# Rounding and splitting the weights by DMA instead of by compute engines, in a hybrid attention and ConvFFN layer

## The chip, the cores and the metric

The kernel runs on one core of a Trainium2 chip. The metric is the device time of one execution in microseconds (us). TensorE (PE in the rows) multiplies; VectorE (DVE), ScalarE (ACT) and GpSimd (POOL) do the elementwise work; SyncE (SP) issues the DMAs, which 16 DMA engines carry out.

## What is computed

One layer of a streaming encoder, on 512 prompt tokens and 32 sample tokens, 544 columns in all:

```python
h = rmsnorm(x, n1)
z = h @ w_in          # q_a | k_a | v_a | q_b | k_b | v_b | gate_a | gate_b
# mixer A: sliding-window attention with sinks; mixer B: chunk-band attention with a bias table
x = x + (sigmoid(gate_a) * o_a + sigmoid(gate_b) * o_b) @ w_out
u = rmsnorm(x, n2) @ w_up
c = conv_b + conv_w[0] * up[:, 0:t] + conv_w[1] * up[:, 1:t+1] + conv_w[2] * up[:, 2:t+2]
a, g = split(c)
x = x + (gelu(a) * g) @ w_down
```

All inputs and outputs are float32; D_MODEL is 1024 and D_FF is 2816.

## The kernel before

**Products in three passes.** The products run on TensorE in a rounded 32-bit type (fp32r). To keep the accuracy of float32, each operand is split into a high half (the value rounded to fp32r) and a low half (the value minus its high half, rounded again), and each product is three matmuls: high times high, high times low, low times high (`triple`, L220). A weight here is one tile of 128 partitions by 1024 elements, 512 KB: one block of 128 output rows over all 1024 inputs. Its product with the activations takes 8 (blocks of the inner dimension) times 2 (halves of the 544 columns, 272 each) times 3, so 48 matmuls.

**Which weights there are.** `sources` lists 110 of them: 52 of `w_in`, 8 of `w_out`, 44 of `w_up` and 6 of `w_down` (the part of `w_down` called `rest`). `ffn` is 60, the number of the first `w_up` weight. The rest of `w_down` is read as `w_pair` by `sums` (L1007), which forms the sums that a fast product of 2 by 2 blocks needs.

**How a weight is prepared.** `prep` (L192) loads the raw tile by a DMA that SP issues, rounds it into `w_hi` (on GpSimd in L201 while `n < ffn`, on ScalarE in L203 after that), and subtracts on VectorE into `w_lo` (L204). The raw tile, `w_hi` and `w_lo` have two buffers each. `weights` (L213) hands out the next weight and sees that the two after it have been asked for (`n + 3`). All of `prep` is traced at a low priority (`LATER`), so the scheduler places its instructions where an engine has nothing more urgent at that point of its plan; the order on each engine is fixed when the kernel is built.

**Stages.** Until about 30 us the input is loaded and normed and the first three weights are used. From there to about 480 us the `w_in` products alternate with attention: each head's norm (`head_norm`, L401), softmax (L478), transposes (`transposed`, L504) and its products are threaded between the dense matmuls by `Stream`, at places that were planned with the constants `LAT_...` and `PACE_...`. Then come `w_out` (to about 520 us), the ConvFFN's `w_up` products, two weights for each tile of the gated value (to about 790 us), the `rest` products (to about 830 us) and the fast product from `sums` (to the end).

**The FFN's pairs.** `make_pair` (L960) splits and sums two gated tiles for the fast product; the first `EARLY` of the 8 pairs are made inside the gate loop, the others after it (L1002).

Of the kernel before, what the change touches and what calls it, by code (L numbers as in the profile page):

```python
# [8 lines left out]
F32 = mybir.dt.float32  # L9
F32R = mybir.dt.float32r  # L10
AF = mybir.ActivationFunctionType
ALU = mybir.AluOpType
# [14 lines left out]
GT = FF // 128  # L27
PAIRS = 8
REST = GT - 2 * PAIRS
EARLY = 5  # L30
UNITS = PAIRS // 2
H = T // 2
EPS = 1e-6
# [24 lines left out]
LAT_SOFT_S, LAT_PTS = 8.46, 1.1  # L58
PACE_A, PACE_B, PACE_S = 7.09, 5.87, 1.44

WARM = 7
START = "x0a w0 x0b x1 w1 x2 w0 x3 w1 x4 x5 x6 x7"
FIRST = 3
# [80 lines left out]
def body(ctx, tc, a, o):  # L144
    nc = tc.nc
    pe = Stream(nc)
    mm, transpose = pe.matmul, pe.transpose
    act = nc.scalar.activation
    V, G = nc.vector, nc.gpsimd
    rr = lambda t: t.bitcast(F32)  # L150

    const = ctx.enter_context(tc.tile_pool(name="const", bufs=1))
    wp = ctx.enter_context(tc.tile_pool(name="wp", bufs=2))
# [12 lines left out]
    def load(out, src, kind="x"):  # L166

        with tc.issue_after(loads[kind].ins) if kind in loads else nullcontext():
            loads[kind] = nc.sync.dma_start(out=out, in_=src)
# [13 lines left out]
    sources = [a["w_in"][m] for m in plan] + [a["w_out"][m] for m in range(8)]  # L183
    ffn = len(sources)
# [4 lines left out]
    W = {}  # L189
    state = {"prepped": 0, "used": 0}  # L190

    def prep(n):  # L192
        raw = wp.tile([128, 1024], F32, name="w_raw", bufs=2)
        hi = wp.tile([128, 1024], F32R, name="w_hi")
        lo = wp.tile([128, 1024], F32R, name="w_lo")
        W[n] = (hi, lo)
        cuts = (0, 256, 1024) if n < 2 else (0, 1024)
        for c in map(slice, cuts, cuts[1:]):
            load(raw[:, c], sources[n][:, c])
            if n < ffn:  # L200
                G.tensor_scalar(hi[:, c], raw[:, c], 1.0, 1.0, ALU.mult, ALU.mult)  # L201
            else:
                nc.scalar.copy(hi[:, c], raw[:, c])  # L203
            V.tensor_tensor(lo[:, c], raw[:, c], rr(hi)[:, c], ALU.subtract)  # L204
            yield

    def prep_next():
        with tc.high_priority(LATER):
            for _ in prep(state["prepped"]):
                pass  # L210
        state["prepped"] += 1

    def weights():  # L213
        n = state["used"]
        state["used"] += 1
        while state["prepped"] < min(n + 3, len(sources)):
            prep_next()
        return W.pop(n)

# [12 lines left out]
    def dense(evac, pool=None):  # L232
        if not norm_done:
            return dense_first(evac)
        if early:
            pool = psa
            early.clear()
        w = weights()
        for s, (c0, cn) in enumerate(HALVES):
            ps = bank(pool or psd)  # L240
            for k in range(KC):
                triple(ps, w, k, c0, cn, k == 0, k == KC - 1)
                if k == KC - 1:
                    evac(s, c0, cn, ps[:, :cn])
                if xt:
                    rescale(state["used"], s, k)
                pe.step()
# [23 lines left out]
    def dense_first(evac):  # L271


        early.append((evac, weights()))
        if len(early) < (FIRST if xt else 2):
            return
        halves = [(bank(psd if i < 3 else psa), early[i // 2][1], i % 2) for i in range(2 * len(early))]
        interleaved(halves[:3], range(KC))
        for h in halves[3:]:
            interleaved([h], range(KC))  # L280
        while not norm_done:
            pe.idle()
        for i, (ps, _, s) in enumerate(halves):
            c0, cn = HALVES[s]
            early[i // 2][0](s, c0, cn, ps[:, :cn])
# [80 lines left out]
    att = ctx.enter_context(ExitStack())  # L366
# [5 lines left out]
    V.memset(rr(zeros)[:, :512], 0.0)  # L372
    for i in range(WARM):
        mm(warm, lhsT=zeros[:, :128], rhs=zeros[:, :512], start=i == 0, stop=i == WARM - 1)

    xt = [slot() for _ in range(KC)]
    load(n1, a["n1"])
    w = [prep(0), prep(1)]
    for step in START.split():
        n = int(step[1])  # L380
        if step[0] == "w":
            next(w[n])
        else:
            c = {"": slice(0, T), "a": slice(0, HALVES[0][1]), "b": slice(HALVES[0][1], T)}[step[2:]]
# [485 lines left out]

    lag = 2
    w0, w1 = weights(), weights()
    halves = [(bank(psd), w0, 0), (bank(psd), w0, 1), (bank(psd), w1, 0), (bank(psa), w1, 1)]
    for k in range(KC):
# [8 lines left out]
    interleaved(halves[3:], range(KC))  # L883
    att.close()

    fp = att.enter_context(tc.tile_pool(name="fp", bufs=50, reuse_waits="tile"))
    ft = att.enter_context(tc.tile_pool(name="ft", bufs=1, reuse_waits="tile"))
    x1 = [fp.tile([128, T], F32, name="s") for _ in range(KC)]
    for m in range(KC):
# [63 lines left out]
    rest, pairs = [], []  # L953
    homes = [gp] * 19 + [fp] * (7 * EARLY + 2 * REST - 19) + [f"x{p}{k}" for k in range(KC) for p in "hl"]

# [4 lines left out]
    def make_pair(v1, v2):  # L960
        b11, b12, b21, b22 = (v[:, c:c + H] for v in (v1, v2) for c in (0, H))
        t13, t24 = (fp.tile([128, T], F32, name="s") for _ in range(2))
        first, *wide = home(), (home(), home()), (home(), home()), (home(), home())
        nc.scalar.copy(first[:, :H], b11)
        V.tensor_tensor(first[:, H:], b11, rr(first)[:, :H], ALU.subtract)
        split(*wide[0], v2)
        V.tensor_tensor(t13[:, :H], b11, b12, ALU.subtract)
        V.tensor_tensor(t13[:, H:], b12, b22, ALU.subtract)
        split(*wide[1], t13)
        V.tensor_tensor(t24[:, :H], b22, t13[:, :H], ALU.add)  # L970
        V.tensor_tensor(t24[:, H:], b21, t24[:, :H], ALU.subtract)
        split(*wide[2], t24)
        ops = {"b11": (first[:, :H], first[:, H:])}
        for names, hl in zip((("b21", "b22"), ("t1", "t3"), ("t2", "t4")), wide):
            for e, name in enumerate(names):
                ops[name] = tuple(x[:, e * H:e * H + H] for x in hl)
        pairs.append(ops)

    late = []
    for n, i in enumerate(gate_order):  # L980
# [6 lines left out]
        def gate(c, part=part, n=n):  # L987
# [7 lines left out]
            late.append(v)  # L995
            if n % 2 and len(pairs) < EARLY:
                make_pair(*late)
# [8 lines left out]

    def sums():  # L1007
        for n in range(KC // 2 * UNITS):
            raw = wp.tile([128, 1024], F32, name="w_raw", bufs=2)
            load(raw, a["w_pair"][n])  # L1010
            wc, wd, wa, wb = (raw[:, 256 * e:256 * e + 256] for e in range(4))
            s13, s24 = (fp.tile([128, 2, 256], F32, name="s") for _ in range(2))
            s1, s3, s2, s4 = s13[:, 0], s13[:, 1], s24[:, 0], s24[:, 1]
            V.tensor_tensor(s13, raw[:, 256:768].rearrange("p (e c) -> p e c", e=2),
                            wc.unsqueeze(1).to_broadcast([128, 2, 256]), ALU.add)
            V.tensor_tensor(s2, s1, wa, ALU.add)
            V.tensor_tensor(s4, s2, wb, ALU.add)
            for x in (wa, s2, s3, s1, wb, wd, s4):
                w = fp.tile([128, 2, 256], F32R, name="s")
                nc.scalar.copy(w[:, 0], x)  # L1020
                V.tensor_tensor(w[:, 1], x, rr(w)[:, 0], ALU.subtract)
                ready.append(w)
                yield

    ready = []
    making = sums()

    def operand(n, ahead=10):
# [9 lines left out]
    def block(n):  # L1038
        if n // 8 not in held:
            held[n // 8] = weights()  # L1040
        hi, lo = held[n // 8]
        ks = slice(128 * (n % 8), 128 * (n % 8) + 128)
        return hi[:, ks], lo[:, ks]

    for m in range(KC):
        ps = [bank(psa if m % 2 else psd) for _ in HALVES]
        for k in range(REST):
            for s, (c0, cn) in enumerate(HALVES):
                hi, lo = block(m * REST + k)
# [182 lines left out]
```

## Time and profile before

| | us |
|---|---|
| median of 3 runs | 924.47 (922.49 to 924.73) |
| the profiled execution | 924.88 |
| its span, from the first to the last instruction | 923.0 |

| engine | busy us | share of the span | instructions |
|---|---|---|---|
| PE | 898.6 | 97% | 7085 |
| DVE | 723.6 | 78% | 1471 |
| ACT | 542.2 | 59% | 1285 |
| POOL | 379.1 | 41% | 578 |

Of the profiled execution, 1.9 us lie around its span. Busy time of TensorE is the time in which at least one of its matmuls is under way; they overlap, so the mean duration of one (292 ns) is longer than the distance from one to the next. A share over the whole span is a mean of stages with different limits, so the stages are read one by one.

### The profile page before, as it was taken

The page shows a single profiled execution, that of the slowest core. Times are in us where ns is not written, and L with a number is a line of the kernel's source. Part 1 is how long each engine was busy: PE and PEld are TensorE (multiplying, and loading weights), DVE is VectorE, ACT ScalarE, POOL GpSimd, SP SyncE. Part 2 cuts the span into 40 slices and gives each one's busy share as a digit, 9 for nine tenths or more (in the row PEclk, how much of TensorE's full clock was granted, in tenths as well). Part 3 has the DMA queues.
Part 4 walks back from the last instruction along what each step waited for, and adds up shares of the span by engine and source line. Part 5 has one row for each costly group of instructions (what it writes and reads, how often), then busy time and mean ns, then how long its engine had stood idle before and what let it go on. Part 6 is the DMA issues. An engine that isn't in the chain of part 4 may idle for free.

```text
span 923.0 us, 18908 instructions
## 1 busy us (share of the span) xinstructions
PE 898.6 (97%) x7085; PEld 884.4 (96%) x7085; DVE 723.6 (78%) x1471; ACT 542.2 (59%) x1285; POOL 379.1 (41%) x578
## 2 busy tenths in 40 slices
PE   8879999999999999999999999999999999999998
PEld 7879899989989999999999999999999999999998
DVE  7799876868888888998866558768777776886996
ACT  5568777778878777777764244344444443534542
POOL 6534457465876777766541103221222221100100
PEclk9999999999999999999999999999999999999999
DMA  6222222322334443434415222222222222332342
GB/s 216 83 82 88 71 90 85 101 81 75 109 118 122 135 124 109 129 110 136 133 59 168 89 92 92 92 77 85 92 93 92 84 87 83 96 101 81 119 145 67
DMA packets 40012, 94.38 MB, mean 102 GB/s; under 512 B 4944, under 2 KB 16240, under 8 KB 39920
## 3 DMA queue, kind: packets, MB, share of 16 engines
q1 hardware_dynamic: 39920, 93.17, 31.8%
q8 instruction: 56, 0.92, 0.4%
q14 instruction: 36, 0.29, 0.1%
HBM read 80.48 MB, written 7.10 MB: 95 GB/s over the span
## 4 chain that ended last, share of the span: by engine, by line
PE 76%; DVE 9%; ACT 4%; POOL 3%; issue 2%; DMA 0%; DVEq 0%; POOLq 0%
PE ps L85 73%; PE ps L89 3%; ACT p L485 2%; DVE q L446 1%; DVE zn L422 1%; DVE p L501 1%; DVE w_lo L204 1%; POOL p L493 1%; DVE s L254 1%; DVE t_b L319 1%; DVE k L431 1%; POOL t_sql L414 1%; POOL z L421 1%; DVE pt_l L512 0%; DMA k<-k 0%
## 5 line engine op out<-in xcount | busy, mean ns | idle before, releaser
L85 PE MATMUL ps<-xh,w_lo 128*128 128x272 f32 x1536 | 446.3, 292 | 5.1 <-DVE w_lo L204 5.1
L85 PE MATMUL ps<-xh,w_hi 128*128 128x272 f32 x1536 | 446.0, 292 | 2.7 <-ACT z L412 1.7
L85 PE MATMUL ps<-xl,w_hi 128*128 128x272 f32 x1536 | 446.3, 291 | 0.8 <-DVE xl L327 0.8
L85 PEld LDWEIGHTS ps<-xh,w_lo 128*128 128x128 f32 x1536 | 291.6, 190 | 6.5 <-DVE w_lo L204 6.0
L85 PEld LDWEIGHTS ps<-xh,w_hi 128*128 128x128 f32 x1536 | 291.5, 190 | 4.8 <-ACT z L412 1.9
L85 PEld LDWEIGHTS ps<-xl,w_hi 128*128 128x128 f32 x1536 | 292.0, 190 | 2.1 <-DVE xl L327 1.7
L204 DVE TENSOR_TENSOR w_lo<-w_raw,w_hi 128x1024 fp32r<-128x1024 f32 (+2 forms) x112 | 143.2, 1279 | 30.8 <-ACT w_hi L203 18.3
L201 POOL TENSOR_SCALAR w_hi<-w_raw 128x1024 fp32r<-128x1024 f32 (+2 forms) x62 | 66.6, 1075 | 90.2 <-PE ps L85 70.3
L493 POOL TENSOR_SCALAR p<-p,rc 128x256 f32<-128x256 f32 (+3 forms) x128 | 74.2, 596 | 41.4 <-DVE rc L491 38.0
L203 ACT CAST w_hi<-w_raw 128x1024 fp32r<-128x1024 f32 x50 | 52.6, 1051 | 64.9 <-issue 36.1
L85 PE MATMUL ps<-s,w_hi 128*128 128x272 f32 x448 | 84.0, 288 | 0.0
L485 ACT ACTIVATE p<-p,nm 128x256 f32<-128x256 f32 (+3 forms) x128 | 65.4, 514 | 27.8 <-DVE nm L482 27.7
L938 POOL TENSOR_SCALAR state_u<-u 128x2 f32<-128x2 f32 x44 | 17.1, 388 | 148.7 <-DVE u L935 148.7
L85 PE MATMUL ps<-s 128*128 128x272 f32 (+1 forms) x483 | 71.3, 293 | 1.7 <-DVE s L372 1.7
L85 PEld LDWEIGHTS ps<-s,w_hi 128*128 128x128 f32 x448 | 70.1, 188 | 0.0
L935 DVE TENSOR_TENSOR u<-ps,rstd 128x272 f32<-128x272 f32 x88 | 38.5, 441 | 39.6 <-PE ps L85 37.0
L85 PEld LDWEIGHTS ps<-s 128*128 128x128 f32 x483 | 65.1, 190 | 2.2 <-DVE s L372 1.7
L85 PE MATMUL ps<-s,w_lo 128*128 128x272 f32 x224 | 63.8, 288 | 0.0
L85 PE MATMUL ps<-k,q 128*128 128x256 f32 (+2 forms) x256 | 52.1, 308 | 3.5 <-DMA k<-k 1.8
L414 POOL TENSOR_TENSOR t_sql<-t_sq,t_sqh 128x272 fp32r<-128x272 f32 x52 | 52.7, 1014 | 3.7
L421 POOL TENSOR_TENSOR z<-z,t_y 128x272 f32<-128x272 f32 x52 | 42.7, 822 | 23.9 <-ACT t_y L316 21.7
L512 DVE TENSOR_TENSOR pt_l<-ps,pt_h 128x512 fp32r<-128x512 f32 (+1 forms) x80 | 45.6, 602 | 5.5 <-ACT pt_h L511 4.4
(166 smaller groups left out, 1635.1 us busy)
## 6 DMA issues: line engine op xcount, KB each, us to landing
w_raw<-in_w_in SPq DMA_DIRECT2D x50, 512.0 KB, 3.4
w_raw<-in_w_up SPq DMA_DIRECT2D x44, 512.0 KB, 3.3
w_raw<-in_w_pair SPq DMA_DIRECT2D x16, 512.0 KB, 3.4
k<-k SPq DMA_DIRECT2D x40, 128.0 KB, 2.3
bias<-in_rel SPq DMA_DIRECT2D x16, 256.0 KB, 2.7
w_raw<-in_w_out SPq DMA_DIRECT2D x8, 512.0 KB, 3.5
s<-in_x SPq DMA_DIRECT2D x15, 272.0 KB, 5.7
w_raw<-in_w_down SPq DMA_DIRECT2D x6, 512.0 KB, 3.3
```

What stands on the lines that cost most here:

```text
L85: return self.nc.tensor.matmul(out, lhsT=lhsT, rhs=rhs, **kw)
L89: return self.nc.tensor.transpose(out, src, ident)
L201: G.tensor_scalar(hi[:, c], raw[:, c], 1.0, 1.0, ALU.mult, ALU.mult)
L203: nc.scalar.copy(hi[:, c], raw[:, c])
L204: V.tensor_tensor(lo[:, c], raw[:, c], rr(hi)[:, c], ALU.subtract)
L414: G.tensor_tensor(sql, sq, rr(sqh), ALU.subtract)
L421: G.tensor_tensor(z, z, y, ALU.mult)
L485: act(p[:, sl], p[:, sl], AF.Exp, bias=nm[:, t:t + 1], accum_out=sm[:, t:t + 1])
L493: G.tensor_scalar(p[:, sl], p[:, sl], rc[:, t:t + 1], 1.0, ALU.mult, ALU.mult)
L512: V.tensor_tensor(l[:, :n], ps[:, :n], rr(h)[:, :n], ALU.subtract)
L935: V.tensor_tensor(u[:, 2 + c0:2 + c0 + cn], ps, rstd2[:, c0:c0 + cn], ALU.mult)
L938: G.tensor_scalar(state_u[:, m, 0:2], u[:, NP:NP + 2], 1.0, 1.0, ALU.mult, ALU.mult)
```

## The change

For the weights from the fifth on (`DIRECT = 4`), `w_hi` is written by a DMA that GpSimd issues and that casts float32 to fp32r, straight from the weight in memory. `w_lo` is then written as minus `w_hi`, by VectorE while `n < ffn` and by ScalarE after that, and a second DMA that GpSimd issues adds the weight from memory into `w_lo`. That adding DMA is held back by one weight: it is issued behind the casting DMA of the next weight. `w_hi` and `w_lo` get four buffers each instead of two, and `weights` asks for `n + 5` instead of `n + 3`. The raw tiles go: the first four weights and `sums` use buffers of `w_hi` for theirs, and `sums` puts its sums into a buffer of `w_lo`. The pool `fp` has 45 tiles instead of 50 and `EARLY` is 4 instead of 5; the scratch space for DMA descriptors that GpSimd writes grows from 1024 to 4096.

```diff
--- before.py
+++ after.py
@@ -27,7 +27,7 @@
 GT = FF // 128
 PAIRS = 8
 REST = GT - 2 * PAIRS
-EARLY = 5
+EARLY = 4
 UNITS = PAIRS // 2
 H = T // 2
 EPS = 1e-6
@@ -58,6 +58,8 @@
 LAT_SOFT_S, LAT_PTS = 8.46, 1.1
 PACE_A, PACE_B, PACE_S = 7.09, 5.87, 1.44
 
+DIRECT = 4
+WBUFS = 4
 WARM = 7
 START = "x0a w0 x0b x1 w1 x2 w0 x3 w1 x4 x5 x6 x7"
 FIRST = 3
@@ -189,20 +191,34 @@
     W = {}
     state = {"prepped": 0, "used": 0}
 
+    cast, held_back = [], []
+
     def prep(n):
-        raw = wp.tile([128, 1024], F32, name="w_raw", bufs=2)
-        hi = wp.tile([128, 1024], F32R, name="w_hi")
-        lo = wp.tile([128, 1024], F32R, name="w_lo")
+        hi = wp.tile([128, 1024], F32R, name="w_hi", bufs=WBUFS)
+        lo = wp.tile([128, 1024], F32R, name="w_lo", bufs=WBUFS)
         W[n] = (hi, lo)
-        cuts = (0, 256, 1024) if n < 2 else (0, 1024)
-        for c in map(slice, cuts, cuts[1:]):
-            load(raw[:, c], sources[n][:, c])
-            if n < ffn:
+        if n < DIRECT:
+            raw = wp.tile([128, 1024], F32, name="w_hi", bufs=WBUFS)
+            cuts = (0, 256, 1024) if n < 2 else (0, 1024)
+            for c in map(slice, cuts, cuts[1:]):
+                load(raw[:, c], sources[n][:, c])
                 G.tensor_scalar(hi[:, c], raw[:, c], 1.0, 1.0, ALU.mult, ALU.mult)
-            else:
-                nc.scalar.copy(hi[:, c], raw[:, c])
-            V.tensor_tensor(lo[:, c], raw[:, c], rr(hi)[:, c], ALU.subtract)
-            yield
+                V.tensor_tensor(lo[:, c], raw[:, c], rr(hi)[:, c], ALU.subtract)
+                yield
+            return
+        with tc.issue_after(cast[-1].ins) if cast else nullcontext():
+            cast.append(G.dma_start(out=hi, in_=sources[n]))
+        if n < ffn:
+            V.tensor_scalar(lo, rr(hi), -1.0, 1.0, ALU.mult, ALU.mult)
+        else:
+            act(lo, rr(hi), AF.Copy, scale=-1.0)
+        held_back.append((lo, sources[n]))
+        if len(held_back) > 1 or n == len(sources) - 1:
+            while len(held_back) > (n < len(sources) - 1):
+                low, src = held_back.pop(0)
+                with tc.issue_after(cast[-1].ins):
+                    G.dma_start(out=low, in_=src, accum_op=ALU.add)
+        yield
 
     def prep_next():
         with tc.high_priority(LATER):
@@ -213,7 +229,7 @@
     def weights():
         n = state["used"]
         state["used"] += 1
-        while state["prepped"] < min(n + 3, len(sources)):
+        while state["prepped"] < min(n + 5, len(sources)):
             prep_next()
         return W.pop(n)
 
@@ -883,7 +899,7 @@
     interleaved(halves[3:], range(KC))
     att.close()
 
-    fp = att.enter_context(tc.tile_pool(name="fp", bufs=50, reuse_waits="tile"))
+    fp = att.enter_context(tc.tile_pool(name="fp", bufs=45, reuse_waits="tile"))
     ft = att.enter_context(tc.tile_pool(name="ft", bufs=1, reuse_waits="tile"))
     x1 = [fp.tile([128, T], F32, name="s") for _ in range(KC)]
     for m in range(KC):
@@ -1006,10 +1022,11 @@
 
     def sums():
         for n in range(KC // 2 * UNITS):
-            raw = wp.tile([128, 1024], F32, name="w_raw", bufs=2)
+            raw = wp.tile([128, 1024], F32, name="w_hi", bufs=WBUFS)
             load(raw, a["w_pair"][n])
             wc, wd, wa, wb = (raw[:, 256 * e:256 * e + 256] for e in range(4))
-            s13, s24 = (fp.tile([128, 2, 256], F32, name="s") for _ in range(2))
+            both = wp.tile([128, 4, 256], F32, name="w_lo", bufs=WBUFS)
+            s13, s24 = both[:, 0:2], both[:, 2:4]
             s1, s3, s2, s4 = s13[:, 0], s13[:, 1], s24[:, 0], s24[:, 1]
             V.tensor_tensor(s13, raw[:, 256:768].rearrange("p (e c) -> p e c", e=2),
                             wc.unsqueeze(1).to_broadcast([128, 2, 256]), ALU.add)
@@ -1200,7 +1217,7 @@
     import concourse.bacc as bacc
     from concourse.bass_utils import run_bass_kernel_spmd
 
-    nc = bacc.Bacc("TRN2", target_bir_lowering=False, num_devices=1, dynamic_dma_scratch_size=1024)
+    nc = bacc.Bacc("TRN2", target_bir_lowering=False, num_devices=1, dynamic_dma_scratch_size=4096)
     arrays, a, o = {}, {}, {}
     for name, v in _layout(inputs).items():
         arrays[f"in_{name}"] = v
```

## Rows read from the trace of the kernel before

**Rows 1.** Busy time by stage: length, PE, PEld, DVE, ACT, POOL, clock, DMA, GB/s.

```profile
20.00:52.00 32.00, 28.18 (x207) 27.29 (x206) 24.97 (x41) 16.52 (x42) 20.63 (x28) 0.95 0.29 81
52.00:110.00 58.00, 52.57 (x403) 50.78 (x402) 53.19 (x121) 43.49 (x112) 25.12 (x37) 0.97 0.27 81
110.00:195.00 85.00, 83.48 (x670) 82.36 (x670) 61.20 (x152) 64.03 (x175) 47.29 (x64) 0.98 0.28 86
195.00:300.00 105.00, 101.56 (x812) 99.36 (x811) 89.45 (x220) 85.53 (x252) 74.16 (x99) 1.00 0.34 104
300.00:400.00 100.00, 97.37 (x780) 94.27 (x779) 86.70 (x181) 76.22 (x217) 72.57 (x87) 1.00 0.42 126
400.00:480.00 80.00, 79.64 (x647) 77.51 (x646) 64.79 (x148) 59.48 (x165) 47.70 (x61) 1.00 0.34 105
570.00:650.00 80.00, 80.00 (x641) 80.00 (x640) 58.04 (x85) 33.24 (x42) 18.55 (x54) 1.00 0.26 86
```

**Rows 2.** Waits of TensorE over the whole span: us, times, longest.

```profile
PE ps L85 <- DVE w_lo L204: 5.1, 4, 2.9
PE ps L85 <- POOL w_hi L201: 1.8, 2, 1.4
```

**Rows 3.** The chain in order of time: start us, us, what; weight pieces, last long run.

```profile
54.48 1.23 DVE w_lo L204
...
158.92 1.18 POOL w_hi L201
...
191.00 1.02 POOL w_hi L201
...
327.64 1.14 DVE w_lo L204
...
479.36 440.39 PE ps L85 x3510
```

**Rows 4.** The page, part 4: the chain's shares of the span by engine.

```profile
PE 76%; DVE 9%; ACT 4%; POOL 3%; issue 2%; DMA 0%; DVEq 0%; POOLq 0%
```

**Rows 5.** Groups by shape, 52 to 480 us, POOL, then DVE.

```profile
L201 POOL TENSOR_SCALAR w_hi<-w_raw 128x1024 fp32r<-128x1024 f32 x46 | 50.4, 1096 | 43.4 <-PE ps L85 38.9 <-issue 4.4
...
L204 DVE TENSOR_TENSOR w_lo<-w_raw,w_hi 128x1024 fp32r<-128x1024 f32 x47 | 62.2, 1323 | 8.5 <-POOL w_hi L201 8.1
```

**Rows 6.** Groups by shape, whole span, DVE: one input against two, 272 elements.

```profile
L361 DVE TENSOR_SCALAR rstd<-rstd 128x272 f32<-128x272 f32 x4 | 1.1, 296 | 0.1
...
L898 DVE TENSOR_TENSOR s<-ps,s 128x272 f32<-128x272 f32 x16 | 6.9, 438 | 14.8 <-PE ps L85 14.7
```

**Rows 7.** SP's instructions on the raw tile: duration min/median/max ns, first and last start.

```profile
L169 SPq DMA_DIRECT2D w_raw<-in_w_up x44: 327/328/328, 518.6 to 777.7; - x44
```

**Rows 8.** DMA queue and weight loads, 570 to 790 us: MB, share, us to landing.

```profile
q1 hardware_dynamic: 5185, 18.88, 26.2%
...
w_raw<-in_w_up SPq DMA_DIRECT2D x35, 512.0 KB, 3.3
```

**Rows 9.** DMA share (after the clock) where it is high: after 480 us, in attention.

```profile
480.00:500.00 20.00, 20.00 (x159) 1.00 0.51 172
...
300.00:315.00 15.00, 13.61 (x124) 13.15 (x123) 12.21 (x23) 11.12 (x33) 10.66 (x13) 1.00 0.55 155
```

**Rows 10.** Groups by shape, 570 to 790 us: the ACT rounding and the DVE subtraction.

```profile
L203 ACT CAST w_hi<-w_raw 128x1024 fp32r<-128x1024 f32 x37 | 38.9, 1051 | 39.2 <-PE ps L85 19.6 <-issue 19.5
...
L204 DVE TENSOR_TENSOR w_lo<-w_raw,w_hi 128x1024 fp32r<-128x1024 f32 x37 | 45.3, 1224 | 10.5 <-ACT w_hi L203 10.5
```

**Rows 11.** Waits of TensorE, 52 to 110 us: us, times, longest.

```profile
PE ps L85 <- DVE w_lo L204: 2.9, 1, 2.9
```

**Rows 12.** POOL in order of time: start us, us, instruction, [idle before <-releaser].

```profile
65.86 1.04 POOL L201 TENSOR_SCALAR w_hi<-w_raw 128x1024 fp32r<-128x1024 f32 x1 [5.90 <-PE ps L85]
```

**Rows 13.** Busy time by stage, the `rest` products at the end of the FFN.

```profile
790.00:830.00 40.00, 40.00 (x321) 40.00 (x320) 34.32 (x66) 16.88 (x28) 3.59 (x10) 1.00 0.30 96
```

**Rows 14.** Groups by line, whole span: the subtractions in splits of 544 columns.

```profile
L431 DVE TENSOR_TENSOR s<-s 128x544 fp32r<-128x544 f32 x31 | 22.8, 742 | 3.3 <-ACT s L430 3.2
```

## The prediction, as it was made before the change was run

> **What bounds the kernel now.** I read the time by stage first. From about 480 us to the end TensorE is busy without a gap: 641 matmuls in 80 us, so 0.125 us each and 6.0 us for the 48 of a weight [rows 1]. The chain says the same: its last long piece is 440 us of matmuls, 3510 of them [rows 3]. No change to the other engines can shorten that half; it can only be spoiled. The attention half, 52 to 480 us, is different. TensorE's columns of the five rows sum to 414.6 of 428 us, so 13.4 us of gaps, and 3.8 us more between 20 and 52 us [rows 1]. Beside it VectorE sums to 355 us (83%), ScalarE to 329 and GpSimd to 267 (62%). That no single engine is full and TensorE still has gaps means that chains of small steps are late by turns. The chain's shares say whose: VectorE 9% of the span (83 us), ScalarE 4%, GpSimd 3% (28 us) [rows 4], nearly all of it ahead of 479 us. So in the 450 us before that, VectorE is what is late for 83/450 = 18% of the time and GpSimd for 28/450 = 6%. Of the gaps, 5.1 us end with a wait for `w_lo` and 1.8 us for `w_hi` [rows 2].
>
> **The change part by part.** Per weight of the attention half (46 between 52 and 480 us) it does this.
>
> VectorE: the subtraction of 1.32 us [rows 5] becomes a sign change with one input. Its price: the subtraction of 272 elements takes 438 ns and of 1024 takes 1224 [rows 6, 10], so 1.045 ns an element and 154 ns fixed; the one-input instruction on 272 elements takes 296 ns [rows 6], so 0.52 ns an element, and 1024 would be 154 + 535 = 0.69 us. No row shows it with an fp32r output, so the bounds are 0.69 and 1.22 us. I take 0.69, the row of the same instruction, plus the 0.1 us by which the subtraction is longer here than in the FFN (1.32 against 1.22, [rows 5, 10]): 0.79. Saved: 0.53 x 46 = 24 us of VectorE's 355. Of that, 18% lies where VectorE is late: -4.4 us (bounds -5.2 and 0). The pieces counted one by one agree: eight pieces of `w_lo` stand on the chain between 54 and 328 us (the first and the last in [rows 3]), and 8 x 0.53 = 4.2.
>
> GpSimd: the rounding of 1.10 us goes, two DMA issues come. No row shows a DMA issued by GpSimd. SP's issue of the same tile takes 0.33 us [rows 7]; GpSimd's own work on a tile of this size 1.10 [rows 5]. Per weight the balance lies between 2 x 0.33 - 1.10 = -0.44 and 2 x 1.10 - 1.10 = +1.10 us, over 46 weights between -20 and +51 us on an engine with 161 us free. I take the upper end, as GpSimd does everything on 128 partitions in about that time; 6% of it is on the path: +3.1 us (bounds -1.2 and +3.1). The Trainium skill, page DMA: Bandwidth & Descriptors, section Latency and other measured facts, puts the emission of a GpSimd DMA's descriptors at about 1 us; by that the issue term would be +2.5 us. No row here shows it.
>
> Buffers: the longest wait for a weight, 2.9 us in 52 to 110 us [rows 11], is of `w_lo` behind a `w_hi` that itself waited 5.9 us for TensorE to leave its buffer [rows 12]; with four buffers that goes. At most 2.9 + 1.8 = 4.7 us (the second being the `w_hi` waits of [rows 2]); but VectorE is busy 53 of 58 us there [rows 1], so the next step in its queue is soon late instead. I take half, -2.2 us (bounds -4.7 and 0).
>
> FFN and `w_out`: ScalarE's rounding of 1.05 us becomes a sign change of the same shape, so nothing; VectorE loses 1.22 us per weight [rows 10], worth nothing where TensorE never waits. What has to hold is the new path of a weight: its buffer comes free when the weight four before it is done (time 0); cast issued, 1.1, landed 3.3 later as the loads do [rows 8], sign change by about 5.5 us; the adding DMA is issued behind the next cast, whose buffer is free at 6.0, so at about 7.1 to 8.2, and lands at 11.5 if it takes as long as a load, at 15 if twice; TensorE wants it three weights later, at 18. So 3 to 6 us of slack, paid for by four buffers; with two it would be late every time. GpSimd is busy 19 of 80 us there [rows 1], so two more issues per 6 us fit. In GpSimd's queue the cast now waits for TensorE and the add for the sign change, and behind them stand the small steps of the convolution and, in attention, the softmax scaling and the norms; the rounding waited for TensorE in the same place (38.9 us in all, [rows 5]), so that wait is old and only the one for the sign change is new.
>
> The end: one `make_pair` moves behind the loop. Its three wide subtractions of 0.74 us [rows 14] and five narrow ones of 0.44 [rows 6], 4.4 us of VectorE, come into a stage where it is busy 34 of 40 us [rows 13], while six subtractions of 1.22 us (7.3) leave it: nothing. `fp` loses five tiles and `sums` takes two fewer from it: nothing.
>
> The sum on the profiled execution: 924.88 - 4.4 + 3.1 - 2.2 = 921.4. The median of the runs lies 0.4 under the profiled one, so 921.0.
>
> **The rivals.** *Even, 924.* The saved VectorE time lies off the path: TensorE's gaps are 13.4 us in all and the plan's launch times do not move. For it: the plan's constants are unchanged, and 82% of the saved time is beside other work by the same chain. Then -2.2 + 3.1, within 1 us of the time before.
>
> *Slower: the sign change waits for the landing.* It stands in VectorE's queue at a place fixed when the kernel was built. Before, the raw tile was loaded long ahead and VectorE waited only 8.1 us for the rounding in the whole half [rows 5]; now cast and sign change share the path of one buffer. If VectorE waits for 3.3 us of flight [rows 8] and the issue of 1.1, that is up to 4.4 us x 46. Its free time after the change is 428 - 331 = 97 us, or 2.1 us a weight: a mean wait over that decides. At 2.5 us it is full and 0.4 x 46 = 18 us over: 924.5 + 18 = 942. Against it: low priority places the sign change late, and by then four buffers have the cast landed.
>
> *Slower: the transfers become the bound of the FFN.* 18.88 MB took 26.2% of 220 us on all 16 engines [rows 8]: 57.6 us for 36 weights, 1.6 us each. Cast and add are 3.2 us if each costs one copy and 4.8 if the add costs two, of 6.0; over 2.75 copies for the add it is full. At three copies, 6.4 us, it loses 0.4 x 50 weights = 20 us: 944; at four, 100 us. In attention and after 480 us the share is up to 0.55 already [rows 9], and there 3.2 us more per weight saturates for some 20 us at a time. No row shows an adding DMA. The Trainium skill, page Collectives: The Full Stack, section The bandwidth ceiling, has reduce-scatter at half the rate of a copy because the add needs two reads; that is the 4.8 us above, and no run here shows it yet.
>
> One rule speaks against the change at another place. [Rows 5, 10] show VectorE's two-input subtraction 0.1 us longer beside a busy GpSimd. The Trainium skill, page SBUF — State Buffer, section Who interferes with whom, says that a one-input VectorE instruction at double rate holds the port pair it shares with GpSimd for its whole length, so that GpSimd cannot write DMA descriptors meanwhile. By it each issue could wait up to 0.69 us, 2 x 46 x 0.69 = 63 us of GpSimd and 6% of that, +4 us: 925, inside the even case.
>
> **How the numbers follow.** Forecast (faster, 921, between 913 with all bounds on the good side, 924.5 - 5.2 - 1.2 - 4.7, and 921.6): 0.40. Even: 0.22. The landing wait, or anything else queued behind the new GpSimd waits, 928 to 955: 0.25. Transfers, 935 to 1020: 0.13. About 0.3% (2.8 us) is what a measurement of this kernel can tell from no change. So faster 0.40, same 0.22, slower 0.38. For the range I leave out the transfers' upper part and the landing wait's last few us (0.15 together) and little below 912: 912 to 950. The likeliest case's own range is 913 to 922.
>
> **What would show it.** Right: sign changes near 0.7 us; VectorE busy some 24 us less in 52 to 480 us; the 2.9 us wait gone; the FFN's DMA share at 0.55 to 0.8 with TensorE at 80.0 of 80 us. Wrong: a wait of VectorE for `w_hi`'s DMA of over 2 us a weight; GpSimd issues over 1.1 us; gaps of TensorE before `w_lo` after 480 us, released by the adding DMA; a plan that comes out in another order in attention, which would move several us either way for reasons that no row here can show.

## The result, and the profile after

The changed kernel takes 951.96 us (median of 4 runs, 951.48 to 953.55) against 923.69 of the kernel before beside it (922.49 to 924.73): ratio 1.031, 95% interval 1.029 to 1.0329. That is 28 us slower, where the prediction said 921.0 and 912 to 950. The profiled spans are 949.9 and 923.0 us, 26.9 apart.

Where the time went is read first from one group of each trace: the products with the high halves of `w_out` and of `rest`, which the trace puts into one group. The first of them is the first product of `w_out`, at the end of attention, the last is the last of `rest`, at the end of the FFN; so "first" and "last" cut the span in three. In order: before, after, and four experiments that come later: e8 (no DMA by GpSimd), e11 (the kernel before with the smaller pools), e2 and e9 (kernels whose attention half is that of the change).

```profile
L85 PE MATMUL ps<-s,w_hi x448: 283/288/297, 486.0 to 835.2; 128*128 128x272 f32 x150
L87 PE MATMUL ps<-s,w_hi x448: 283/288/297, 507.6 to 859.0; 128*128 128x272 f32 x150
L87 PE MATMUL ps<-s,w_hi x448: 283/288/340, 491.3 to 841.5; 128*128 128x272 f32 x150
L85 PE MATMUL ps<-s,w_hi x448: 283/288/297, 483.6 to 832.8; 128*128 128x272 f32 x150
L87 PE MATMUL ps<-s,w_hi x448: 283/288/297, 504.0 to 855.8; 128*128 128x272 f32 x150
L87 PE MATMUL ps<-s,w_hi x448: 283/288/297, 504.4 to 856.4; 128*128 128x272 f32 x150
```

After minus before: attention ends 21.6 us later (507.6 against 486.0), `w_out` and the FFN take 2.2 longer (351.4 against 349.2), the end 3.1 longer (949.9 - 859.0 = 90.9 against 87.8). Four fifths of the loss lie in the attention half. Those are profiles of one execution each: in e2 and e9, whose engines run the same instructions in the same order up to about 530 us, attention ends 18.0 and 18.4 us later than before. Busy time by stage, columns as in [rows 1]:

```profile
52.00:110.00 58.00, 51.64 (x373) 49.22 (x371) 42.00 (x116) 40.80 (x106) 24.75 (x40) 0.93 0.71 151
110.00:195.00 85.00, 82.04 (x638) 79.56 (x639) 54.97 (x149) 64.77 (x178) 47.38 (x72) 0.97 0.62 136
195.00:300.00 105.00, 98.86 (x776) 95.81 (x775) 76.00 (x198) 79.92 (x237) 69.97 (x106) 0.98 0.67 150
300.00:400.00 100.00, 92.58 (x708) 88.50 (x707) 76.75 (x175) 71.13 (x202) 64.67 (x91) 0.97 0.67 162
400.00:480.00 80.00, 77.36 (x615) 75.51 (x614) 60.03 (x149) 57.67 (x170) 48.38 (x73) 1.00 0.70 168
570.00:650.00 80.00, 80.00 (x641) 80.00 (x640) 42.41 (x71) 34.63 (x43) 35.66 (x84) 1.00 0.84 180
```

VectorE did get its relief: 309.8 us busy in 52 to 480 against 355. That is more than the 24 us forecast because the attention half now takes longer: these rows hold 3110 matmuls, those of before 3312, so 6% of the work has moved out of them, some 22 of VectorE's 45 us. TensorE nevertheless has 25.5 us of gaps there, not 13.4, and a lower clock (0.93 to 0.98 up to 400 us, before 0.97 to 1.00). In the FFN TensorE is as full as before, 641 matmuls in 80 us, with the DMA engines at 0.84. So the prediction's guarded place, the FFN, held, and the place with the expected gain lost. One sign of being wrong did show in small, at `w_out`: TensorE's only wait for a weight after attention, released by an adding DMA.

```profile
L87 PE MATMUL ps<-s,w_lo 128*128 128x272 f32 x224 | 64.5, 289 | 0.7 <-DMA w_lo<-in_w_out 0.7
```

The groups of the new path in 52 to 480 us, columns as in [rows 5]; then the issues of the DMA view over the whole span (count, KB, median us to landing), and two of the kernel before:

```profile
L212 DVE TENSOR_SCALAR w_lo<-w_hi 128x1024 fp32r<-128x1024 f32 x44 | 34.1, 774 | 48.3 <-DMA w_hi<-in_w_in 46.4 <-PE ps L87 1.8
L210 POOL DMA_DIRECT2D w_hi<-in_w_in x43 | 26.2, 609 | 52.4 <-PE ps L87 52.4
L220 POOL DMA_DIRECT2D w_lo<-in_w_in x44 | 40.6, 922 | 4.9 <-DVE w_lo L212 2.6 <-DVE mx L517 1.6 <-issue 0.2
```

```profile
w_hi<-in_w_in POOLq DMA_DIRECT2D x48, 512.0 KB, 4.5
w_lo<-in_w_in POOLq DMA_DIRECT2D x48, 512.0 KB, 8.1
k<-k SPq DMA_DIRECT2D x40, 128.0 KB, 5.2
bias<-in_rel SPq DMA_DIRECT2D x16, 256.0 KB, 4.2
```

```profile
k<-k SPq DMA_DIRECT2D x40, 128.0 KB, 2.3
bias<-in_rel SPq DMA_DIRECT2D x16, 256.0 KB, 2.7
```

The sign change costs 0.774 us, the cast's issue 0.61 and the add's 0.92: prices at or under what I took. What is new is the idle time in front of the sign change, 46.4 us in 27 waits, all released by the landing cast. And DMAs that the change does not touch land later: the copies of `k` after 5.2 us (before 2.3), the bias after 4.2 (before 2.7).

**What one such wait does.** VectorE between 53 and 58 us, in order of time, then TensorE there (two lines of it), then five stretches of 2 us (the DMA share counts a transfer's whole time in the row in which it starts, so a short row can show more than 1):

```profile
53.32 0.50 DVE L447 TENSOR_TENSOR ks_lo<-zn,ks_hi 64x32 fp32r<-64x32 f32 x2
56.30 0.69 DVE L212 TENSOR_SCALAR w_lo<-w_hi 128x1024 fp32r<-128x1024 f32 x1 [2.48 <-DMA w_hi<-in_w_in]
56.91 0.49 DVE L335 SCALAR_TENSOR_TENSOR t_b<-ps,eps,t_b 128x272 f32<-128x272 f32 x1
```

```profile
55.40 0.29 PE L87 MATMUL ps<-xl,w_hi 128*128 128x272 f32 x1
57.55 0.38 PE L87 MATMUL ps<-t_sqh,bdiag 128*128 128x272 f32 x1 [1.86 <-DVE t_b L335]
```

```profile
54.00:56.00 2.00, 1.69 (x14) 1.47 (x12) 0.00 (x0) 2.00 (x7) 2.00 (x3) 1.00 0.92 198
56.00:58.00 2.00, 0.45 (x3) 0.48 (x4) 1.70 (x4) 0.55 (x2) 1.41 (x3) 0.94 1.04 239
58.00:60.00 2.00, 2.00 (x11) 2.00 (x11) 2.00 (x6) 0.83 (x2) 1.08 (x2) 0.50 1.15 220
60.00:62.00 2.00, 2.00 (x13) 2.00 (x13) 1.94 (x4) 1.89 (x6) 0.00 (x0) 0.71 1.21 213
62.00:64.00 2.00, 2.00 (x18) 2.00 (x17) 1.91 (x5) 1.99 (x3) 0.00 (x0) 1.00 1.13 237
```

VectorE has nothing to do for 2.48 us but may not go past the sign change. Behind it stands `t_b` of the next norm; TensorE stands 1.86 us for that, not for any weight. After this gap TensorE's granted clock falls to 0.50, its level of 1.2 GHz, and 11 and 13 matmuls go through in 2 us instead of 18. So VectorE's wait of 2.48 us costs TensorE 1.86 us of idle time, and 12 matmuls fewer than 36 in the four us after it, another 1.5 at 0.125 each.

Summed over all rows of 2 us from 16 us to the first `w_out` product (235 before, 245 after): idle time 17.5 and 28.0 us; busy time times the missing share of the clock 4.9 and 13.5 us, in 3 and 7 such drops. Together +19.1 of the +21.6 us. So 8.6 of the 21.6 us, two fifths, went with a lower clock in this execution. In e2 and e9 it is less, 6.5 and 4.9 us of 18.0 and 18.4, in 6 and 5 drops. Not every gap is followed by a drop: after gaps of 2.19 us (at 182 us) and 2.11 (at 475) the clock of the changed kernel stays at 1.00, and the first of its seven drops, at 16 us, comes before GpSimd's first DMA (29.3 us).

### The profile page after: what moved, and what is told of

Read it like the earlier page. It is cut to its first block, busy times and chain, and to the rows that moved or that the text cites. A ratio compares the mean times of both kernels' runs of the same rounds, so it can differ in the third digit from the quotient of the medians.

```text
span 949.9 us, 19018 instructions
## 1 busy us (share of the span) xinstructions
PE 911.1 (96%) x7085; PEld 891.9 (94%) x7085; DVE 625.7 (66%) x1421; ACT 541.2 (57%) x1285; POOL 443.5 (47%) x734
## 4 chain that ended last, share of the span: by engine, by line
PE 43%; issue 2%; DMA 2%; DVE 2%; POOL 1%; ACT 1%; DVEq 0%; POOLq 0%; SPq 0%; ACTq 0%
PE ps L87 43%; DMA w_hi<-in_w_pair 1%; DMA w_lo<-in_w_out 1%; POOL p L509 1%; DVE s L1038 0%; ACT p L501 0%; DVE qs_lo L447 0%; DVE w_lo L1031 0%; POOL w_lo L220 0%; PE ps L91 0%; POOL s L843 0%; POOL w_hi L210 0%; DVE p L517 0%; POOL carry L945 0%; DVE w_lo L1034 0%
## 5 line engine op out<-in xcount | busy, mean ns | idle before, releaser
L214 ACT ACTIVATE w_lo<-w_hi 128x1024 fp32r<-128x1024 f32 x50 | 53.0, 1061 | 138.8 <-DMA w_hi<-in_w_up 95.7
L212 DVE TENSOR_SCALAR w_lo<-w_hi 128x1024 fp32r<-128x1024 f32 x56 | 44.1, 787 | 69.3 <-DMA w_hi<-in_w_in 55.4
L509 POOL TENSOR_SCALAR p<-p,rc 128x256 f32<-128x256 f32 (+3 forms) x128 | 71.1, 619 | 37.5 <-DVE rc L507 31.1
L210 POOL DMA_DIRECT2D w_hi<-in_w_up x44 | 25.4, 577 | 115.5 <-PE ps L87 115.5
L87 PE MATMUL ps<-s 128*128 128x272 f32 (+1 forms) x483 | 67.5, 295 | 2.0 <-DVE s L388 1.8
L87 PE MATMUL ps<-k,q 128*128 128x256 f32 (+2 forms) x256 | 55.4, 313 | 9.7 <-DMA k<-k 6.5
L958 DVE SCALAR_TENSOR_TENSOR s<-u,cols,s 128x544 f32<-128x544 f32 x44 | 34.5, 785 | 40.6 <-ACT s L957 40.6
L437 POOL TENSOR_TENSOR z<-z,t_y 128x272 f32<-128x272 f32 x52 | 48.7, 938 | 21.7 <-ACT t_y L332 21.6
L210 POOL DMA_DIRECT2D w_hi<-in_w_in x48 | 30.1, 627 | 54.0 <-PE ps L87 53.0
L91 PE MATMUL ps<-ident,p 128*128 128x128 f32 x272 | 47.1, 280 | 6.6 <-DVE pt_l L528 3.3
```

Source lines behind the costliest of these rows:

```text
L87: return self.nc.tensor.matmul(out, lhsT=lhsT, rhs=rhs, **kw)
L91: return self.nc.tensor.transpose(out, src, ident)
L210: cast.append(G.dma_start(out=hi, in_=sources[n]))
L212: V.tensor_scalar(lo, rr(hi), -1.0, 1.0, ALU.mult, ALU.mult)
L214: act(lo, rr(hi), AF.Copy, scale=-1.0)
L437: G.tensor_tensor(z, z, y, ALU.mult)
```

## The experiments

In the code cuts of this section `...` marks lines left out. The theory after the first reading: the sign change waits at its fixed place for a cast that lands late because the adds fill the DMA engines. Three rivals: the transfers as such (the FFN, late `k` copies); the buffers and pools; and the order of the work, which the kernel's planner and scheduler set anew for any edit.

**Where it is lost: e1 and e2.** One half of the kernel each with the DMA path, the other half through raw tiles.

```diff
 e1:  -DIRECT = 4          +DIRECT = 60
 e2:  -if n < DIRECT:      +if n < DIRECT or n >= ffn:
      ...
```

> The DMA path for w_up and w_down alone: the 60 weights of w_in and w_out are rounded by GpSimd and subtracted by VectorE as before the change; buffers, pools, EARLY and sums stay as changed. Whole output is computed. Read from the two traces: the first w_out product of the changed kernel on ScalarE's split tiles starts at 507.6 us against 486.0, the last at 859.0 against 835.2, the end is 949.9 against 923.0. Theory that the attention half carries the loss (21.6 us) and FFN (2.2) and end (3.1) the rest: 924 + 5 = 927 to 931. Theory that the transfers of the FFN hurt and the attention half only shows an earlier delay: 945 or more.

> The other half of the split: the DMA path for w_in and w_out alone, the FFN's weights rounded by ScalarE and subtracted by VectorE through raw tiles that share the buffers of w_hi. Whole output is computed. Attention theory: 944 to 949. FFN theory: 925 to 930.

e1: 947.7 us, ratio 1.0263 (1.0241 to 1.0285). e2: 950.74, ratio 1.031 (1.0264 to 1.0357). e2 lies just above its range, and the two do not add up. e2 has nearly all of the loss: its attention half is the changed kernel's, order included, its first `w_out` product comes at 504.0 us (after: 507.6), and its FFN weights are prepared as before. But e1 loses nearly as much without one DMA by GpSimd in attention: there the first `w_out` product comes 7.3 us late, at 493.3, and then one wait stands that the changed kernel does not have.

```profile
PE ps L87 <- DVE s L914: 10.1, 1, 10.1
```

VectorE's addition of the residual waited for a tile of `x` until 516 us; the clock is 0.72 in 500 to 520 us. SyncE issued those loads of `x` only from 512.5 us: in its queue they stood behind loads of `w_out`, which waited for a buffer of `w_hi`. In e1 raw tiles and high halves share these four buffers while five weights are asked for, so this wait is e1's own. So e1 does not price the FFN's transfers. It says something else: a kernel whose attention has the same operations as before came out 7 us worse there, by its buffers, its order or both. The next runs had to hold that apart.

**Landing wait and traffic: e3, e4, e5.** In e3 the attention half's sign change reads the previous weight's high half (`last[0]`), so that it does not wait for its own cast; in e4 the add covers 64 of the 1024 columns; e5 has both edits.

```diff
 e3:  ...
      -V.tensor_scalar(lo, rr(hi), -1.0, 1.0, ALU.mult, ALU.mult)
      +V.tensor_scalar(lo, rr(last[0]), -1.0, 1.0, ALU.mult, ALU.mult)
 e4:  -G.dma_start(out=low, in_=src, accum_op=ALU.add)
      +G.dma_start(out=low[:, :64], in_=src[:, :64], accum_op=ALU.add)
```

> In the attention half the sign change reads the high half of the weight before, which has landed long ago, so VectorE does not wait for the casting DMA; every instruction, transfer and other wait stays. What it leaves out: the low halves of w_in and w_out come out wrong. Theory of the landing wait (VectorE idle 46.4 us before the sign change in 52 to 510 us): most of the 21.6 us of the attention half comes back, 930 to 938. Theory of the transfers (other DMAs land later: the copies of k in 5.2 us instead of 2.3): 947 or more, with k's landing still at 5 us.

> The adding DMA adds 64 of the 1024 columns, so nearly all of its traffic goes, while every instruction and wait stays. What it leaves out: 960 of 1024 columns of the low halves keep minus the high half. Theory of the transfers: most of the 21.6 us comes back, 930 to 938, k's copies land in about 2.5 us. Theory of the landing wait: the cast still takes 4 us or more to land, 942 to 949.

> Both edits at once: the sign change of w_in and w_out reads the high half of the weight before, and the adding DMA adds 64 of 1024 columns. What it leaves out: the low halves come out wrong. If the transfers and the landing wait are two causes that add up (12 us came back without the wait, 22 us without the traffic, of 21.6 in the attention half), this is faster than the kernel before: 910 to 921. If the wait hurts only because the traffic makes the landing late, it equals the run with the small add: 927 to 935.

e3: 937.62, ratio 1.0154 (1.013 to 1.0179). e4: 933.68 (929.15 to 934.49), ratio 1.0102 (1.007 to 1.0134). e5: 933.05, ratio 1.0101 (1.0086 to 1.0117). Without the wait 14 us come back, without the traffic 18, without both 19. So the two do not add up: with the traffic gone, taking the wait away too is worth 0.6 us, which is within the scatter. But e3's order parts from the changed kernel's at 32 us, so its 14 us are wait and order together. VectorE's waits for the cast in 52 to 510 us, after, then e4, then e3:

```profile
DVE w_lo L212 <- DMA w_hi<-in_w_in: 46.4, 27, 4.6
```

```profile
DVE w_lo L212 <- DMA w_hi<-in_w_in: 21.2, 19, 3.9
```

```profile
DVE w_lo L214 <- DMA w_hi<-in_w_in: 3.4, 1, 3.4
```

In e4 the casts land after 3.9 us, the `k` copies after 2.6 and the bias after 2.6, about as before.

Two pairs of these kernels can be compared with the order held fixed. After and e4 hold the same instructions in the same order on VectorE up to about 266 us (the other engines to about there as well), and so do e3 and e5; before and e11 do through all of attention, but for a few small instructions of VectorE and GpSimd in the first 25 us. The same instruction of VectorE at an early and at a late place, after and then e4:

```profile
50.83 0.43 DVE L306 TENSOR_TENSOR s<-ps,rstd 128x272 f32<-128x272 f32 x1
266.46 0.51 DVE L447 TENSOR_TENSOR k<-zn,k 64x272 fp32r<-64x272 f32 x1
```

```profile
48.39 0.43 DVE L306 TENSOR_TENSOR s<-ps,rstd 128x272 f32<-128x272 f32 x1
258.20 0.50 DVE L447 TENSOR_TENSOR k<-zn,k 64x272 fp32r<-64x272 f32 x1
```

e3 and then e5:

```profile
77.32 0.50 DVE L345 SCALAR_TENSOR_TENSOR xl<-s,n,xh 128x272 fp32r<-128x272 f32 x1
259.10 0.86 DVE L449 TENSOR_TENSOR qs_lo<-zn,qs_hi 64x32 fp32r<-64x32 f32 x2
```

```profile
76.13 0.66 DVE L345 SCALAR_TENSOR_TENSOR xl<-s,n,xh 128x272 fp32r<-128x272 f32 x1
255.49 0.87 DVE L449 TENSOR_TENSOR qs_lo<-zn,qs_hi 64x32 fp32r<-64x32 f32 x2
```

The distance of after and e4 grows from 2.4 to 8.3 us, by 5.8; that of e3 and e5 from 1.2 to 3.6, by 2.4; that of before and e11 between the same times not at all (2.23 at 53 us, 2.22 at 257; it arises at the start of the program). These are profiles of single executions, and e4's is the fastest of its runs; what counts is the growth, not the distance. With e2 and e9 in the place of after, the same program in attention, the growth is 4.5 and 5.2 us. Within one order, then, the adds' traffic costs 2.4 us in this stretch where no sign change waits, and 4.5 to 5.8 in the order where it does. At the place shown above, e4 has 1.20 us of VectorE's wait in place of 2.48, 0.3 of TensorE's in place of 1.86, and the clock stays at 1.00. Past 266 us the orders of after and e4 part. So the mechanism is shown for some 5 of the 20 us by which attention is late; how the rest splits between the adds, the wait and the order these runs don't settle.

**A wait that could not be moved: e9.** The sign change held back behind the next weight's cast.

```diff
-        if n < ffn:
+        if n < ffn - 1:
+            pass
+        elif n < ffn:
...
+        if held_back and n < ffn:
+            V.tensor_scalar(held_back[0][0], rr(held_back[0][2]), -1.0, 1.0, ALU.mult, ALU.mult)
```

> The kernel of the change, with the sign change of the attention weights held back by one weight: it is issued behind the next weight's cast, as the add already is. Nothing is left out and the traffic is the same. If the loss beside the traffic is VectorE standing at its place in the queue until the cast lands, this wins back most of what reading the previous weight's tile won (952 to 938): 936 to 942, with VectorE's wait for w_hi's DMA under 10 us. Rival: that gain came from another order in the plan; then this one comes out anywhere, and with the wait gone the time may still be 945 to 955. Rival: the adds now come later and TensorE waits for w_lo in attention instead: gaps before w_lo of over 5 us.

952.56 us, ratio 1.0319 (1.0284 to 1.0354): a miss, and not the test it was meant to be. The scheduler put the sign change at the same place: VectorE's order is that of the changed kernel up to 531 us, and TensorE's, ScalarE's and GpSimd's are to the end. VectorE still waits 38.5 us in 25 waits for the cast between 52 and 510 us. So e9 moved nothing and says nothing for or against the theory; its use is that it repeats the changed kernel's attention.

**The order alone: e6, e7, e10.** One constant of the planner, the flight time it reckons for the copies of `k`, in the changed kernel (e6) and in the kernel before (e7, e10).

```diff
-LAT_SQ, LAT_NORM, LAT_DMA = 2.9, 6.89, 3.63
+LAT_SQ, LAT_NORM, LAT_DMA = 2.9, 6.89, 6.5     (e10: 4.5)
```

> The changed kernel with the plan's constant for the copies of k raised from 3.63 to 6.5 us (they land in 5.2 us instead of 2.3 and TensorE waits 6.5 us for them). Whole output is computed. If late copies of k are a main path of the loss: 938 to 944 and TensorE's wait for k gone. If the loss goes through VectorE and the weights: 948 to 953.

> The kernel before with the same constant raised to 6.5 us: a control for what another order of the plan alone does to the time, without any DMA from GpSimd. Whole output is computed. If the order of the plan is worth little: 922 to 926. If plans scatter by as much as the losses under dispute: more than 5 us away, on either side.

> The kernel before with the planner's constant for a DMA's flight at 4.5 instead of 3.63 us: no work, buffer or engine changes, only the order in attention. A second look at what another order alone does (6.5 gave 935.7). If the order before is a lucky one among many, this one is slower too, 928 to 938. If 6.5 cost 12 us because so large a constant starts steps too late, 4.5 costs a third of it or less: 924 to 928.

e6: 957.5, ratio 1.037 (1.0351 to 1.0389). e7: 935.7, ratio 1.0137 (1.012 to 1.0155). e10: 935.43, ratio 1.0136 (1.0111 to 1.016). e6 lies above both of its ranges. A later launch did not cure the late `k` copies: TensorE's wait for them fell from 6.5 to 3.1 us in e6, VectorE's for the casts from 46.4 to 26.7, and the time rose. So where the order changes, the sum of these waits doesn't give the time. The two controls are the more useful result. They have the operations, buffers and traffic of the kernel before, and lose 12 us; and they lose the same with the constant a quarter larger and four fifths larger, so not in proportion to it. The order of the kernel before is better than either of these neighbours, and any edit that makes the planner start over in attention risks about 10 us.

**Buffers, pools, and everything but the DMAs: e8, e11, e12.** e8 is the changed kernel with all weights through raw tiles and engines (its raw tiles take part of the four buffers of `w_hi`, as in the change only the first four weights' do). e11 is the kernel before with `EARLY` 4 and 45 tiles of `fp`. e12 adds to e11 a third buffer for each half.

```diff
 e8:  -DIRECT = 4    +DIRECT = 110      -n + 5    +n + 3    ...
 e11: -EARLY = 5     +EARLY = 4         -name="fp", bufs=50   +name="fp", bufs=45
 e12: as e11, and    -name="w_hi")      +name="w_hi", bufs=3)     (w_lo too)
```

> No DMA from GpSimd at all: all 110 weights are rounded and subtracted as before, two asked for ahead, but with the buffers of the change (raw tiles in the four buffers of w_hi, four of w_lo, fp 45, EARLY 4, sums in w_hi and w_lo). Whole output is computed. If buffers and pools are innocent: 922 to 926. If they carry the 7 us by which the attention half was late with the DMA path in the FFN alone, and the 2 to 3 us at the end: 930 to 934.

> The kernel before with the smaller pools of the change alone: one make_pair fewer inside the loop (EARLY 4 for 5), 45 tiles of fp for 50. The order in attention is the same as before. I predicted nothing for this term: 923 to 925. If the moved make_pair or the tiles that are lacking cost something, it shows at the end of the kernel, in 840 to 925 us: up to 928.

> As the run with the smaller pools, and three buffers of each high and low half instead of two (two raw tiles as before): the buffer term of the prediction alone, GpSimd and VectorE as before. The prediction's term was -2.2 us with bounds -4.7 and 0: 919 to 924. If it is another order in attention that decides, and the order before is a lucky one, 928 to 938 in spite of the freed buffers.

e8: 933.14, ratio 1.0109 (1.0094 to 1.0124). e11: 929.94, ratio 1.0073 (1.005 to 1.0096). e12: 941.47, ratio 1.0204 (1.0179 to 1.023). Three results. The frame of the change without its DMAs costs 9 to 10 us. The smaller pools, which I had costed at nothing, cost 7 by themselves, beyond what was expected of e11 and all behind attention: from the first `w_out` product to the end 444.8 us against 437.0 (928.4 - 483.6, 923.0 - 486.0). Whether the moved `make_pair` or the five missing tiles cost it was not run apart. And the buffers, which I had at -2.2 us, bring no gain that survives the new order: e12, above both of its ranges, is 11.5 us slower than e11, its first `w_out` product 13.1 us later (496.7 against 483.6). The end of e11 in the chain of waits, the pieces of over 0.9 us:

```profile
829.97 22.65 PE ps L85 x164
...
852.64 1.69 PE ps L85 x8
...
854.80 1.24 DVE s L1021 x2
...
858.75 2.19 DMA out_y<-s
...
861.48 19.39 PE ps L85 x152
...
882.61 42.50 PE ps L85 x334
```

In the kernel before the last piece of [rows 3], TensorE without a wait, runs through this place. Here an output must leave before its tile of `fp` is free. TensorE stands idle only 3.1 of the 7.8 us for such steps; about half of the rest is in the first piece, 164 matmuls in 22.65 us, 0.138 us each in place of 0.125, and why they come slower there no run shows. The changed kernel and e8 have their own form of it, as their sums use the weights' buffers: in the changed kernel the chain runs through loads of `w_pair` into `w_hi`.

```profile
859.36 3.38 DMA w_hi<-in_w_pair
867.87 3.25 DMA w_hi<-in_w_pair
873.60 3.81 DMA w_hi<-in_w_pair
878.87 1.53 PE ps L87 x10
```

**The sum of the runs.** From 923.7: frame without DMAs 933.1 (e8, +9 to 10: pools and sums at the end, buffers, order); casts in place of GpSimd's roundings and sign changes in place of subtractions, little of the adds' traffic and hardly a wait, 933.05 (e5, nothing); the adds' traffic 937.6 (e3, +4.6); the landing wait under that traffic 952.0 (+14.3). Each of the four steps also changes the order, except the third up to about 290 us, so these are differences between kernels and not prices of causes. No kernel here beats the one before.

## Why the prediction was wrong

Two steps failed. The landing wait was to decide only once VectorE would be full; it held TensorE up long before that. And the new order in attention was named but left out of the sum, while another order alone moves this kernel by 12 us. A third, the end, was put at nothing and took 3 us. How the loss in attention splits between wait, traffic and order stays open.

**What bounds the kernel.** Right in that the second half could only be spoiled, and it was hardly touched. Wrong in what followed for the first half: I read "chains of small steps are late by turns" and then worked with averages over 450 us.

**VectorE, -4.4 us.** The price was right (0.79 forecast, 0.774 measured), the place was not. The 18% came from the chain of one order. e5 has the whole relief (and little traffic, and 1.7 us of that wait left) and equals e8, which has none of it: 933.05 and 933.14. So no gain is seen, and 0 was the term's other bound; but the two kernels also differ in their order, which can hide a gain of this size, so the term itself was not measured. The share of a chain says whose step was late in the order that ran; the change put another order in its place.

**GpSimd, +3.1 us.** Two issues cost 0.61 + 0.92 = 1.53 us, not 2.2, against the 1.10 that goes; the term would be +1.2 by the same working. The reason given for the upper end, that GpSimd does everything on 128 partitions in about 1.1 us, was a misreading: in the kernel before, the means of its larger groups on 128 partitions in attention run from 0.58 us (L413) to 1.44 (L827). The Trainium skill, DMA: Bandwidth & Descriptors, section Latency and other measured facts, has about 1 us for the emission; the mean here is 0.77. Of the stall of up to 0.69 us that I weighed against the change, by the Trainium skill, SBUF — State Buffer, section Who interferes with whom, little is seen: the mean of 44 add issues lies 3 ns above their median of 919, and that 45 above the shortest, 874; the longest is 1.32 us.

**Buffers, -2.2 us.** Wrong in sign as far as e12 can tell: +11.5 with the order that came with them. The wait of [rows 11] did go, in the changed kernel as in e12, but its 2.9 us are less than what a new order moves.

**FFN, nothing; transfers as a rival.** The guarded step held but for the 0.7 us at `w_out`. The DMA share of 0.84 over 5.99 us per weight (48 x 80/641) is 5.0 us, less 1.6 for the cast if it costs what the load did, so 3.4 for the add. From e4: the DMA-queue share in 570 to 790 us is 34.2% there and 82.9% after, 2.9 us a weight for the 960 columns left out, so 3.1 for all. By both estimates the add takes about two copies, as in the rival's 4.8 us. That agrees with the Trainium skill, Collectives: The Full Stack, section The bandwidth ceiling, where the add of a reduce-scatter needs two reads. Cast and add land after 5.2 and 7.6 us, and the four buffers cover that: 80.00 of 80 us.

**The end, nothing.** Mis-sized: 3.1 us in the changed kernel, 7.8 in e11. I reckoned the moved subtractions against VectorE's free time and did not ask what the missing tiles and the shared buffers hold up: the chains above run through an output's flight and a load's.

**The landing wait, the rival at 942.** The right mechanism with the wrong point of decision. I let it decide only once VectorE would be full, over 2.1 us a weight. It is 46.4/44 = 1.05 us a weight, VectorE is at 72%, and yet one wait of 2.48 us took 1.86 us from TensorE; taking the waits away with the same traffic gives 14 us, with another order. The wait need not fill the engine; it need only stand ahead of the one small step that TensorE wants next. I also had its cause by halves: I took 3.3 us of flight and treated the transfers as the FFN's matter, while in attention the DMA share rose to 0.62 to 0.71 and casts landed 0.6 us later at the median than without the adds' traffic (e4), copies of `k` 2.6 later. "Low priority places the sign change late, and by then four buffers have the cast landed" was the sentence that failed: the casts themselves waited 52.4 us in all for TensorE to leave their buffers, and the order had not moved the sign change far enough behind it: 27 of 44 sign changes waited for the landing.

**The order.** My last sentence named it and gave it neither a price nor a chance. e7 and e10 show what it can cost, about 12 us to the slower side, larger than every term of my sum. That was the main gap in the chances: a sum of 4 us between states whose order differs cannot carry "faster" at 0.40.

## What to carry to other kernels

A wait in an in-order queue is priced by what stands behind it, not by the engine's free time: look at the next few instructions and who waits for them, and add what TensorE loses in clock after the gap. Where a planner or scheduler sets the order anew, run a control that changes the order alone before a term of a few microseconds is believed, and compare kernels over the stretch in which their queues hold the same order. A transfer that an idle resource seems to give for nothing can be paid by the small copies that share it.

## What the runs showed of the hardware that was not expected

- After a gap of TensorE of 1.9 us the granted clock was 0.50 for the next 2 us and 0.71 for the 2 after; after two other gaps, of 2.1 and 2.2 us, it stayed at 1.00. The changed kernel has 7 such drops before the first `w_out` product against 3, worth 8.6 us more; two repeats of the same order have 6 and 5, worth 6.5 and 4.9.
- An adding DMA of 512 KB takes the DMA engines for about two copies (3.1 to 3.4 us against 1.6, an estimate from the shares) and lands after 8.1 us in attention and 7.6 in the FFN; the rounding one lands after 4.5 and 5.2.
- Beside them the smaller transfers of another queue are delayed more: 128 KB of `k` land in 5.2 us instead of 2.6 in e4, 256 KB of bias in 4.2 instead of 2.6, while the casts themselves go from 3.9 to 4.5.
- GpSimd issues an adding DMA in 0.92 us and a casting one in 0.61.
